# The first loads of a weight gradient: half of slice 1's X goes to a hardware queue, slice 0's narrow G to the software queue

## Chip, core and metric

The kernel runs on one core of one Trainium2 chip. The metric is the device time of one execution in microseconds (us); the time before is the median of four runs.

Engines are named as in the profile: PE multiplies matrices, PEld is its weight load (it overlaps PE), DVE and ACT copy, cast and add, POOL issues the loads of the software queue and SP and ACT those of the hardware queues. DMA engines, 16 of them, move the data of all queues.

## What is computed

```python
batch, m, k, n = 16, 512, 1024, 768
# input: (batch, m, k) float32, grad_output: (batch, m, n) float32
grad_weight = np.einsum('bmk,bmn->kn', input, grad_output)
```

With X as 8192 x 1024 and G as 8192 x 768 this is the product X^T G, 1024 x 768, summed over 8192 rows.

## The kernel before

**Slices.** The 8192 rows are cut into 64 slices (S) of 128 rows. A slice of X is 128 x 1024, a slice of G 128 x 768. Matmuls are in bfloat16 with float32 sums; inputs arrive in float32, so every slice has to be cast.

**Three parts of the output.** The first 512 columns of the output ("wide", columns of G below NA) are made in 8 groups of 128 rows: four groups are part A (they read the first half of X), four are part B (the second half of X). The last 256 columns ("narrow") are made turned over, with narrow G as the weights and X as the moving data, in 4 groups: part N. N's groups take the second half of X first. So a slice costs 4 matmuls in each of A, B and N, each 128 x 128 by 128 x 512, and 12 in all.

**Banks and the order.** There are 8 banks to sum in and 12 groups. The list ORDER (lines 17 to 20) says in which order parts are worked: "A2" brings part A up to slice 2 (slices are counted from 0, so that is slices 0 and 1), and a "!" closes it, that is, its banks are copied (first time, lines 120 to 124, DVE and ACT in turns) or added (later, line 118, DVE) to sums in SBUF and go back to the end of the list of free banks. Before: A1! N1 B2! N2 A2 N3! and so on. The instructions of PE, DVE and ACT run in the order in which they are written (line 67).

**Loads.** Two ways lead in. SP and ACT each own a hardware queue, which copies float32 as it is: slice 0 comes this way (lines 70 to 75), wide G and then narrow G on SP, the two halves of X on ACT, and DVE and ACT cast it (line 106, called from lines 108 to 115). POOL owns the software queue, which casts to bfloat16 on the way: slices 1 to 63 come this way (lines 90 to 97), G before X, and slice 1's X in two halves, the second first. A software load is issued when the one eight places before it has landed; up to eight are under way.

**Before and after.** PE first runs 12 matmuls on constants (line 81) while the first loads are under way. At the end the last 14 slices of A and B are summed group by group (lines 228 to 240), and each group is stored as it is ready.

Of the kernel before, what the change touches and what calls it, by code (L numbers as in the profile page):

```python
# [8 lines left out]
P = 128  # L9
NA = 512  # L10
# [4 lines left out]


ORDER = (
    "A1! N1 B2! N2 A2 N3! A3 B3 A4! B5 N5 B6! N7 A6 N8! A9! B10 N9 B12! N12! A12! "
    "B15 AB17! n17! AB26! n26! AB41! n41! AB47 A50! B50! N64!"
).split()  # L20

# [5 lines left out]
def kernel(  # L27
# [6 lines left out]
    nc = tc.nc  # L34
    bf16 = mybir.dt.bfloat16
    f32 = mybir.dt.float32

    B, M, K = input.shape
    _, _, N = grad_output.shape
    S = B * M // P  # L40
# [5 lines left out]
    X = input.rearrange("b m k -> (b m) k")  # L46
    G = grad_output.rearrange("b m n -> (b m) n")
    OUT = out.rearrange("(ks p) n -> p ks n", p=P)

    head = ctx.enter_context(tc.tile_pool(name="head", bufs=1))  # L50
    xg = ctx.enter_context(tc.tile_pool(name="xg", bufs=XBUFS))
# [10 lines left out]
    xs = [None] * S  # L62
    gwide = [None] * S
    gnarrow = [None] * S
# [2 lines left out]
    ctx.enter_context(tc.manual_schedule(engines={E.PE, E.DVE, E.Activation}))  # L67


    xf = head.tile([P, K], f32, name="xf")  # L70
    gf = head.tile([P, N], f32, name="gf")
    nc.sync.dma_start(out=gf[:, 0:NA], in_=G[0:P, 0:NA])
    nc.scalar.dma_start(out=xf[:, 0:NA], in_=X[0:P, 0:NA])
    nc.sync.dma_start(out=gf[:, NA:N], in_=G[0:P, NA:N])
    nc.scalar.dma_start(out=xf[:, NA:K], in_=X[0:P, NA:K])


    ones = nc.const_aps.tensor(1.0, (P, P), bf16)
# [8 lines left out]
        )  # L87


    for s in range(1, S):  # L90
        gt = xg.tile([P, N], bf16, name="gt")
        nc.gpsimd.dma_start(out=gt, in_=G[s * P : (s + 1) * P, :])  # L92
        xs[s] = xg.tile([P, K], bf16, name="xt")
        for c0, c1 in ((NA, K), (0, NA)) if s == 1 else ((0, K),):
            nc.gpsimd.dma_start(out=xs[s][:, c0:c1], in_=X[s * P : (s + 1) * P, c0:c1])  # L95
        gwide[s] = gt[:, 0:NA]
        gnarrow[s] = gt[:, NA:N]

    xs[0] = head.tile([P, K], bf16, name="x0")
    g0 = head.tile([P, N], bf16, name="g0")  # L100
    gwide[0] = g0[:, 0:NA]
    gnarrow[0] = g0[:, NA:N]

    def round_by(engine, dst, src, c0, c1):
        copy = nc.vector.tensor_copy if engine == "DVE" else nc.scalar.copy
        copy(out=dst[:, c0:c1], in_=src[:, c0:c1])  # L106

    round_by("DVE", g0, gf, 0, 304)
    round_by("ACT", g0, gf, 304, NA)
    for k in range(0, KS // 2, 2):  # L110
        round_by("DVE", xs[0], xf, k * P, (k + 1) * P)
        round_by("ACT", xs[0], xf, (k + 1) * P, (k + 2) * P)
    round_by("DVE", g0, gf, NA, N)
    round_by("DVE", xs[0], xf, NA, 6 * P)
    round_by("ACT", xs[0], xf, 6 * P, K)

    def add_out(dst, src):
        nc.vector.tensor_add(out=dst, in0=src, in1=dst)  # L118
# [68 lines left out]
    def slice_by_slice(names, upto, close):  # L187
        while any(parts[n].done < upto for n in names):
            for n in names:
                part = parts[n]  # L190
                s = part.done
                if s == upto:
                    continue
                part.done += 1
                first = not part.banks
                for i in range(len(part.groups)):
                    if first:
                        open_bank(part, i)
                for i in range(len(part.groups)):
                    add_slice(part, i, s, first, close and s == upto - 1)  # L200

    def bank_by_bank(part, upto):
        first = part.done
        part.done = upto
        for i in range(len(part.groups)):
            open_bank(part, i)
            for s in range(first, upto):
                add_slice(part, i, s, s == first, s == upto - 1)

    for step in ORDER:  # L210
        close = step.endswith("!")
        names = step.rstrip("!").rstrip("0123456789")
        upto = int(step.rstrip("!").lstrip("ABNn"))
        if names.islower():
            bank_by_bank(parts[names.upper()], upto)
        else:
            slice_by_slice(names, upto, close)

    rows_of = out.rearrange("(b r) n -> r b n", r=SQ)
    for a in range(P // SQ):  # L220
        c = NA + a * NT * SQ
        nc.scalar.dma_start(
            out=rows_of[:, :, c : c + NT * SQ],
            in_=turned[a * SQ : (a + 1) * SQ].rearrange("p b r t -> p b (r t)"),
# [3 lines left out]
    for k in range(KS):  # L228
        slices = range(parts["A" if k < KS // 2 else "B"].done, S)
        pieces = [(0, NA)] if k < KS - 1 else [(0, 256), (256, 384), (384, NA)]  # L230
        for c0, c1 in pieces:
            name = free.pop(0)
# [38 lines left out]
```

## Time and profile before

| | us |
|---|---|
| median of 4 runs (176.39 to 176.66) | 176.52 |
| profiled execution, its own time | 176.26 |
| its span (first to last instruction) | 174.5 |
| PE busy | 169.3 |
| first matmul on data (A, slice 0) starts | 4.87 |
| last load of the software queue issued by POOL | 137.0 |
| bytes read from HBM | 58.72 MB |

The span is what the trace covers; the time of the execution has 1.8 us more around it. The granted clock of TensorE is 0.999. Of the DMA engines' time, 90.7% of the span goes to the software queue's packets and 4.4% and 3.9% to the two hardware queues. In rows of the profile, xf and gf are the float32 tiles of slice 0, x and g their bfloat16 copies, and xt and gt the bfloat16 tiles of the software queue.

### The profile page before, as it was taken

What the parts mean: (1) busy time and instruction counts of PE and PEld (TensorE: products, weight loads), DVE (VectorE), ACT (ScalarE), POOL (GpSimd) and SP (SyncE); (2) the same over time, 40 slices, a digit from 0 to 9 for tenths busy, and PEclk for the clock granted to TensorE, in tenths of its full rate; (3) what the DMA queues carried; (4) which work ended last, traced back from release to release, by engine and by line L of the source; (5) the groups of instructions that cost most, each with busy time, mean ns of one, the idle gap of its engine ahead of it and who ended that gap; (6) DMA issues with size and microseconds to landing.
All of it is one profiled execution on the core that took longest, in us unless ns stands there. A gap on an engine that the chain in (4) does not pass through costs nothing.

```text
span 174.5 us, 2012 instructions
## 1 busy us (share of the span) xinstructions
PE 169.3 (97%) x793; PEld 78.0 (45%) x808; DVE 60.9 (35%) x101; ACT 5.6 (3%) x11; POOL 67.4 (39%) x131
## 2 busy tenths in 40 slices
PE   8899999999999999999999999999999999999993
PEld 3344444444444444444444444444444444444463
DVE  0645582882940039300000662200460003932122
ACT  2540000000000000000000000000000000000000
POOL 7544444444445444444444444444264200000000
PEclk9999999999999999999999999999999999999999
DMA  5999999999999999999999999999999991084913
GB/s 159 224 208 209 208 208 208 209 208 208 208 209 209 207 208 209 209 209 208 208 208 209 207 211 207 208 208 208 208 208 209 208 207 22 0 188 130 225 62 120
DMA packets 25336, 33.09 MB, mean 190 GB/s; under 512 B 6512, under 2 KB 16880, under 8 KB 25328
## 3 DMA queue, kind: packets, MB, share of 16 engines
q0 software_dynamic: 18288, 28.91, 90.7%
q1 hardware_dynamic: 2592, 2.49, 4.4%
q10 hardware_dynamic: 4448, 1.57, 3.9%
q8 instruction: 6, 0.10, 0.2%
q14 instruction: 2, 0.02, 0.0%
HBM read 58.72 MB, written 3.15 MB: 355 GB/s over the span
## 4 chain that ended last, share of the span: by engine, by line
PE 80%; DMA 15%; POOL 2%; issue 1%; DVE 0%; POOLq 0%
PE bank L127 53%; PE bank L134 27%; DMA xt<-in_input_dram 15%; POOL gt L92 1%; POOL xt L95 1%; DVE acc L118 0%; POOLq L255 0%
## 5 line engine op out<-in xcount | busy, mean ns | idle before, releaser
L127 PE MATMUL bank<-gt,xt 128*128 128x512 bf16 (+2 forms) x523 | 110.6, 368 | 0.6 <-DMA xt<-in_input_dram 0.2
L127 PEld LDWEIGHTS <-xt 128*128 128x128 bf16 x532 | 50.8, 98 | 58.8 <-DMA xt<-in_input_dram 1.2
L118 DVE TENSOR_TENSOR acc<-bank,acc 128x512 f32<-128x512 f32 (+2 forms) x62 | 37.9, 665 | 73.8 <-PE bank L127 73.4
L134 PE MATMUL bank<-xt,gt 128*128 128x512 bf16 x246 | 55.9, 379 | 0.3
L95 POOL DMA_DIRECT2D xt<-in_input_dram x64 | 33.9, 531 | 37.6 <-DMA xt<-in_input_dram 36.1
L92 POOL DMA_DIRECT2D gt<-in_grad_output_dram x63 | 33.6, 533 | 32.4 <-DMA gt<-in_grad_output_dram 26.0
L134 PEld LDWEIGHTS <-gt 128*128 128x128 bf16 x252 | 24.6, 98 | 29.9 <-issue 0.4
L118 DVE TENSOR_TENSOR acct<-bank,acct 128x512 f32<-128x512 f32 x24 | 15.7, 681 | 30.1 <-PE bank L134 30.0
L81 PE MATMUL bank<-const-bfloat16-1.0 128*128 128x512 bf16 (+1 forms) x12 | 3.6, 468 | 0.8 <-PEq L255 0.8
L122 DVE COPY acc<-bank 128x512 f32<-128x512 f32 x4 | 2.6, 684 | 1.1 <-PE bank L127 1.1
L178 DVE STREAM_TRANSPOSE turned<-acct 128x512 f32<-128x512 f32 x4 | 2.9, 714 | 0.1
L81 PEld LDWEIGHTS <-const-bfloat16-1.0 128*128 128x128 bf16 x12 | 1.4, 124 | 2.8 <-issue 2.4
L127 PE MATMUL bank<-g,x 128*128 128x512 bf16 x8 | 2.1, 380 | 0.5 <-DVE x L106 0.5
L124 ACT COPY acc<-bank 128x512 f32<-128x512 f32 x4 | 2.1, 586 | 1.4 <-PE bank L127 1.4
L106 DVE CAST g<-gf 128x304 bf16<-128x304 f32 (+1 forms) x2 | 0.6, 318 | 4.3 <-DMA gf<-in_grad_output_dram 4.3
L122 DVE COPY acct<-bank 128x512 f32<-128x512 f32 x2 | 1.3, 686 | 1.3 <-PE bank L134 1.3
L127 PEld LDWEIGHTS <-x 128*128 128x128 bf16 x8 | 0.8, 97 | 1.3 <-DVE x L106 0.7
L106 ACT ACT_TABLE_LOAD x1 | 1.3, 1283 | 1.7 <-PEq L255 1.7
L124 ACT COPY acct<-bank 128x512 f32<-128x512 f32 x2 | 1.1, 589 | 1.6 <-PE bank L134 1.6
L134 PE MATMUL bank<-x,g 128*128 128x512 bf16 x4 | 1.0, 377 | 0.1
L106 ACT CAST x<-xf 128x128 bf16<-128x128 f32 (+1 forms) x3 | 0.9, 330 | 0.4 <-DMA xf<-in_input_dram 0.4
L106 DVE CAST x<-xf 128x128 bf16<-128x128 f32 (+1 forms) x3 | 0.8, 295 | 0.2 <-DMA xf<-in_input_dram 0.2
(6 smaller groups left out, 1.2 us busy)
## 6 DMA issues: line engine op xcount, KB each, us to landing
xt<-in_input_dram POOLq DMA_DIRECT2D x62, 256.0 KB, 8.5
gt<-in_grad_output_dram POOLq DMA_DIRECT2D x63, 192.0 KB, 8.5
out_dram<-acc SPq DMA_DIRECT2D x13, 128.0 KB, 3.0
out_dram<-turned ACTq DMA_DIRECT2D x4, 256.0 KB, 3.5
xf<-in_input_dram ACTq DMA_DIRECT2D x2, 256.0 KB, 4.1
gf<-in_grad_output_dram SPq DMA_DIRECT2D x1, 256.0 KB, 3.6
xt<-in_input_dram POOLq DMA_DIRECT2D x2, 128.0 KB, 5.7
out_dram<-acc SPq DMA_DIRECT2D x1, 256.0 KB, 2.0
```

Source lines behind the costliest of these rows:

```text
L81: nc.tensor.matmul(wps[:, 0:cols], ones, nc.const_aps.tensor(1.0, (P, cols), bf16), start=True, stop=True,)
L92: nc.gpsimd.dma_start(out=gt, in_=G[s * P : (s + 1) * P, :])
L95: nc.gpsimd.dma_start(out=xs[s][:, c0:c1], in_=X[s * P : (s + 1) * P, c0:c1])
L106: copy(out=dst[:, c0:c1], in_=src[:, c0:c1])
L118: nc.vector.tensor_add(out=dst, in0=src, in1=dst)
L122: nc.vector.tensor_copy(out=dst, in_=src)
L124: nc.scalar.copy(out=dst, in_=src)
L127: nc.tensor.matmul(bank, xs[s][:, k * P : (k + 1) * P], gwide[s][:, c0:c1], start=start, stop=stop)
L134: nc.tensor.matmul(bank, gnarrow[s].rearrange("p (r t) -> p t r", t=NT)[:, t], xs[s][:, h * NA : (h + 1) * NA], start=start, stop=stop,)
L178: nc.vector.transpose(out=turned[:, h * hb : (h + 1) * hb, :, t], in_=dst.rearrange("p (b r) -> p b r", r=SQ),)
```

## The change

SP's hardware queue still brings slice 0's wide G first; its second load is now the second half of slice 1's X (float32, rows of 2 KB) in place of slice 0's narrow G (rows of 1 KB). ACT's queue is unchanged. The software queue starts with slice 0's narrow G, then slice 1's G and the first half of slice 1's X; from slice 2 on it is as before. Slice 1's second half of X is cast by DVE and ACT, and these casts stand in their order behind the evictions of A1!. Narrow G of slice 0 needs no cast any more. In ORDER a step B1 stands between A1! and N1, so that PE works A, B, N on slice 0 where it was A, N, B; N then sums in the banks that A has left. Slice 1's X no longer uses a buffer of the ring of X tiles.

```diff
 ORDER = (
-    "A1! N1 B2! N2 A2 N3! A3 B3 A4! B5 N5 B6! N7 A6 N8! A9! B10 N9 B12! N12! A12! "
+    "A1! B1 N1 B2! N2 A2 N3! A3 B3 A4! B5 N5 B6! N7 A6 N8! A9! B10 N9 B12! N12! A12! "
...
-    xf = head.tile([P, K], f32, name="xf")
-    gf = head.tile([P, N], f32, name="gf")
-    nc.sync.dma_start(out=gf[:, 0:NA], in_=G[0:P, 0:NA])
-    nc.scalar.dma_start(out=xf[:, 0:NA], in_=X[0:P, 0:NA])
-    nc.sync.dma_start(out=gf[:, NA:N], in_=G[0:P, NA:N])
-    nc.scalar.dma_start(out=xf[:, NA:K], in_=X[0:P, NA:K])
+    xf = [head.tile([P, K], f32, name=f"xf{s}") for s in range(2)]
+    gf = head.tile([P, NA], f32, name="gf")
+    nc.sync.dma_start(out=gf, in_=G[0:P, 0:NA])
+    nc.scalar.dma_start(out=xf[0][:, 0:NA], in_=X[0:P, 0:NA])
+    nc.sync.dma_start(out=xf[1][:, NA:K], in_=X[P : 2 * P, NA:K])
+    nc.scalar.dma_start(out=xf[0][:, NA:K], in_=X[0:P, NA:K])
...
-    for s in range(1, S):
-        gt = xg.tile([P, N], bf16, name="gt")
-        nc.gpsimd.dma_start(out=gt, in_=G[s * P : (s + 1) * P, :])
-        xs[s] = xg.tile([P, K], bf16, name="xt")
-        for c0, c1 in ((NA, K), (0, NA)) if s == 1 else ((0, K),):
-            nc.gpsimd.dma_start(out=xs[s][:, c0:c1], in_=X[s * P : (s + 1) * P, c0:c1])
+    for s in range(S):
+        pool = head if s == 0 else xg
+        gt = pool.tile([P, N], bf16, name="gt")
+        pool = head if s < 2 else xg
+        xs[s] = pool.tile([P, K], bf16, name=f"x{s}" if s < 2 else "xt")
         gwide[s] = gt[:, 0:NA]
         gnarrow[s] = gt[:, NA:N]
...
+        g0 = NA if s == 0 else 0
+        nc.gpsimd.dma_start(out=gt[:, g0:N], in_=G[s * P : (s + 1) * P, g0:N])
+        if s > 0:
+            x1 = NA if s == 1 else K
+            nc.gpsimd.dma_start(out=xs[s][:, 0:x1], in_=X[s * P : (s + 1) * P, 0:x1])
...
-    round_by("DVE", g0, gf, NA, N)
-    round_by("DVE", xs[0], xf, NA, 6 * P)
-    round_by("ACT", xs[0], xf, 6 * P, K)
+    round_by("DVE", xs[0], xf[0], NA, 6 * P)
+    round_by("ACT", xs[0], xf[0], 6 * P, K)
...
-    for step in ORDER:
+    for i, step in enumerate(ORDER):
+        if i == 1:
+            round_by("DVE", xs[1], xf[1], NA, 6 * P)
+            round_by("ACT", xs[1], xf[1], 6 * P, K)
```

More of the change, by code (lines that the diff above doesn't have):

```diff
@@ L87 @@
         )
-    for s in range(1, S):
-        gt = xg.tile([P, N], bf16, name="gt")
-        nc.gpsimd.dma_start(out=gt, in_=G[s * P : (s + 1) * P, :])
-        xs[s] = xg.tile([P, K], bf16, name="xt")
-        for c0, c1 in ((NA, K), (0, NA)) if s == 1 else ((0, K),):
-            nc.gpsimd.dma_start(out=xs[s][:, c0:c1], in_=X[s * P : (s + 1) * P, c0:c1])
+    for s in range(S):
[3 more added lines that the diff above has]
+        xs[s] = pool.tile([P, K], bf16, name=f"x{s}" if s < 2 else "xt")
         gwide[s] = gt[:, 0:NA]
         gnarrow[s] = gt[:, NA:N]
[L99 to L102, printed above, removed]
+        g0 = NA if s == 0 else 0
[3 more added lines that the diff above has]
+            nc.gpsimd.dma_start(out=xs[s][:, 0:x1], in_=X[s * P : (s + 1) * P, 0:x1])
     def round_by(engine, dst, src, c0, c1):
@@ L106, in round_by @@
         copy(out=dst[:, c0:c1], in_=src[:, c0:c1])
-    round_by("DVE", g0, gf, 0, 304)
-    round_by("ACT", g0, gf, 304, NA)
+    round_by("DVE", gwide[0], gf, 0, 304)
+    round_by("ACT", gwide[0], gf, 304, NA)
     for k in range(0, KS // 2, 2):
-        round_by("DVE", xs[0], xf, k * P, (k + 1) * P)
-        round_by("ACT", xs[0], xf, (k + 1) * P, (k + 2) * P)
-    round_by("DVE", g0, gf, NA, N)
-    round_by("DVE", xs[0], xf, NA, 6 * P)
-    round_by("ACT", xs[0], xf, 6 * P, K)
+        round_by("DVE", xs[0], xf[0], k * P, (k + 1) * P)
+        round_by("ACT", xs[0], xf[0], (k + 1) * P, (k + 2) * P)
+    round_by("DVE", xs[0], xf[0], NA, 6 * P)
+    round_by("ACT", xs[0], xf[0], 6 * P, K)
     def add_out(dst, src):
```

## The prediction

> **What bounds the kernel now.** I read the busy shares first, then the chain of waits, then PE's stalls one by one, then the data queues of the first 8 us.
>
> ```profile
> PE 169.3 (97%) x793; PEld 78.0 (45%) x808; DVE 60.9 (35%) x101; ACT 5.6 (3%) x11; POOL 67.4 (39%) x131
> ```
>
> ```profile
> 4.48 8.04 DMA xt<-in_input_dram
> 12.53 0.28 issue
> 12.81 8.55 DMA xt<-in_input_dram
> 21.36 0.28 issue
> 21.64 9.04 DMA xt<-in_input_dram
> 30.68 0.05 issue
> 30.73 1.04 PE bank L127 x4
> ```
>
> PE is busy 97% of the span, and the chain that ended last has two parts. Up to 30.68 us it runs over software-queue loads: an X load lands, the next issue that waited for its semaphore goes out, and that one lands 9 us later. From 30.73 us to the last add at 171.73 us it is PE alone, with no wait. So whatever the change does counts by one thing: when the matmul that now starts at 30.73 us (step B12, slice 11) can start. It starts when slice 11's X has landed (30.68 us). Everything behind it is 141 us of matmuls that the change leaves as they are.
>
> ```profile
> 4.87 1.04 PE L127 MATMUL bank<-g,x 128*128 128x512 bf16 x4 [0.52 <-DVE x L106]
> 6.01 1.02 PE L134 MATMUL bank<-x,g 128*128 128x512 bf16 x4
> 6.87 1.03 PE L127 MATMUL bank<-g,x 128*128 128x512 bf16 x4
> 7.73 1.03 PE L127 MATMUL bank<-gt,xt 128*128 128x512 bf16 x4
> ...
> 30.73 1.04 PE L127 MATMUL bank<-gt,xt 128*128 128x512 bf16 x4 [0.16 <-DMA xt<-in_input_dram]
> ```
>
> (PE's instructions in order of time.) Matmuls start 0.216 us apart, so four take 0.86 us. From the single starts, PE loses between 4.87 and 30.73 us: 0.27 us before N1 (6.01), 0.05 at 10.38, 0.10 at 14.79, 0.07 at 19.18 and 0.32 at 30.73; 0.81 us in all. The last four each begin right behind the landing of X of slice 2 (10.33), 4 (14.74), 6 (19.14) and 11 (30.68). Gaps of 0.43 us at every 50th matmul are missing records, not stalls. That 0.81 us is all that any change in the loads can win once the first matmul has started.
>
> The first stall is this one:
>
> ```profile
> 5.55 0.40 ACT L106 CAST x<-xf 128x256 bf16<-128x256 f32 x1 [0.45 <-DMA xf<-in_input_dram]
> 5.55 0.29 DVE L106 CAST x<-xf 128x256 bf16<-128x256 f32 x1 [0.24 <-DMA xf<-in_input_dram]
> ```
>
> The second half of slice 0's X lands at 5.53 us, the casts end at 5.84 on DVE and 5.95 on ACT, and N1 needs both.
>
> **The data queues.** Busy time by stretch (length, engines, granted clock, DMA share, GB/s):
>
> ```profile
> 3.00:4.00 1.00, 1.00 (x5) 0.36 (x4) 0.00 (x0) 0.00 (x0) 1.00 (x3) 1.00 0.97 328
> 4.00:4.80 0.80, 0.35 (x4) 0.16 (x2) 0.46 (x3) 0.46 (x2) 0.80 (x3) 1.00 1.09 407
> ...
> 6.00:8.00 2.00, 1.99 (x10) 0.92 (x10) 1.04 (x2) 0.93 (x2) 0.77 (x2) 1.00 1.17 190
> ```
>
> GB/s counts bytes written. Up to 4.8 us the hardware queues copy float32, so 407 written is 407 read. Afterwards the software queue writes bfloat16: 190 (208 in the slices of the steady stretch) written is 380 to 416 read. So a byte costs the engines the same on either queue. The packet records say it finer: a 2 KB row is followed by the next on its engine after 80 ns on both kinds of queue, a 1 KB row (narrow G, hardware) after 42 ns, a 3 KB row after 116 ns. They also show the order: an engine does wide G and the first half of X, then the 8 rows of narrow G, then the 8 of the second half of X, and its first software packet (4.82 to 5.16 us, engine by engine) starts some 6 ns after its last hardware packet. The software queue, issued from 1.23 us on, stands behind the hardware queues.
>
> **The change, part by part.** Let d be the shift of the software stream at slice 11's X.
>
> (1) Hardware queues: SP's second load is 256 KB (half of X of slice 1) in place of 128 KB of narrow G. Per engine 8 rows of 80 ns for 8 of 42 ns: +0.30 us; from the stretch at 407 GB/s 131 KB are +0.32 us, at the 328 of 3 to 4 us +0.40. I take +0.32. Two things move with it. The second half of slice 0's X, served behind SP's second load, lands at 5.83 to 5.85 us and not 5.53. And the software queue starts 0.3 us later on each engine.
>
> (2) Software queue: out goes half of X of slice 1 (8 rows of 80 ns an engine, 0.65 us), in comes narrow G of slice 0 (1 KB read, 512 B written). No such row runs in this queue. By bytes read it is like the hardware's narrow row, 42 ns, 0.34 us; from above, a packet that costs what the 1 KB-written one does, 80 ns, 0.64 us. So -0.31 us to 0.00. I take 46 ns: the row that reads the same bytes is the nearest, and software packets of 2, 3 and 4 KB read go at 80, 116 and 156 ns, a line that has almost no fixed part. That is -0.28 us. The number of issues on POOL (each 0.53 us) and the eight loads in flight stay the same, so nothing else in the stream moves.
>
> d = +0.32 - 0.28, about **+0.03 us** (between 0.00 and +0.40 by these ends). In other words: slices 0 to 11 must all have been read before that matmul, the same bytes at the same rate, and only their order among slices 0 and 1 changes.
>
> (3) PE order A1 B1 N1 B2 for A1 N1 B1 B2. B1 needs the late half of X, which N1 needed too. Casts start at 5.85, DVE's ends at 6.14, and with 0.06 us to the weight load (5.84 to 5.90 now) B1 starts at 6.20, where N1 now starts at 6.01; ACT's half (6.25) is wanted at 6.6. So PE is 0.19 us later and not earlier: N1 7.06, B2 7.93, N2 8.79, A2 9.65, N3 10.52. Narrow G lands near 6.2 to 6.4 (first software load now 6.43 us, 0.93 us of packets; later start +0.3, shorter by 0.6), well before 7.06.
>
> (4) Casts removed: DVE's narrow-G cast (0.29 us at 5.01), while DVE then waits for X anyway: nothing. Casts added: slice 1's half, DVE 0.29, ACT 0.40. They stand behind A1's evictions (2 x 0.64 on DVE, 2 x 0.53 on ACT, from 6.06, for DVE starts the next 0.08 us before an end, and from 6.25), so DVE 7.34 to 7.63, ACT 7.31 to 7.71, with their data landed near 5.8. B2 loads weights at 7.72: 0.05 us of wait at most. Behind them stand B2's evictions, wanted from 8.3: free. N1 now takes A1's banks: third bank free at 7.34, wanted at 7.49. This cover is thin; 0.3 us more on the casts would put 0.2 us on N1 or B2.
>
> (5) What becomes of PE's lag: it meets the old stalls. At 10.38 the lag is 0.14, at 14.79 it has eaten the wait of 0.10 and 0.04 is left, at 19.18 nothing. Without any wait for loads PE could be at the B12 matmul at 30.73 - 0.54 + 0.19 = 30.38 us; the load says 30.73 + d. The later one rules, so the lag costs nothing until B1 is another 0.35 us late, and no gain in the stream beyond 0.35 us is usable.
>
> Sum: the profiled execution took 176.26 us (span 174.5); +0.03 makes 176.29. The median of the runs is 176.52, 0.26 above the profiled one, so the forecast is **176.55 us**: no change. A difference below 0.2% (0.35 us) is about what a measurement of this kernel can't tell from none.
>
> **The rivals.** *Small packets hold up the software queue (slower).* Place: narrow G at the head of the queue. For: its X half at the head, the load it replaces, was itself slow to land: the last engine's landing came 1.05 us after wide G's (6.43 to 7.48), the next half's 0.65 later, and single packets there took up to 280 ns for 98. Against: the median engine lost only 0.07. Price: 0.65 to 1.05 us for narrow G where I put 0.37, so d of +0.31 to +0.71; it leaves the 0.2% at about 86 ns a packet. With 0.50 it gives 177.05 us.
>
> *The stream gets ahead (faster).* The same hiccup read the other way: without that half in the software queue up to 0.40 us of it is gone for good. For: two engines carry the delay on to 23.5 us (last landings 0.4 to 0.5 behind the median). Against: slice 11's last landing is another engine's, delayed by a 0.9 us instruction fetch at 23.75 us (its landings trail the others' by 0.5 us from then on). Capped by PE at 0.35, or at 0.40 if the engines happen to serve slice 0's half first, so that B1 isn't late: 176.15 us, at the edge of the 0.2%.
>
> *The queues share (PE becomes the bound).* If software packets mix with the longer hardware queue, the second half of slice 0's X is late by another 8 x 80 ns, B1 starts near 6.84, PE reaches the B12 matmul at 31.02: +0.29 us, 176.8. Against: 16 of 16 engines hand over cleanly now. The Trainium skill ("DMA: Bandwidth & Descriptors", Queues, rings and completion order) says that an engine goes round-robin between the queues that have work, a whole packet of descriptors at a time; by that rule this case is the regular one, and the trace doesn't bear it out for these loads unless the software descriptors were late.
>
> *That it does as its order suggests* (B1 covering N1's wait) needs the late half of X on time; 0.27 us is the most there, and the load of slice 11 takes it back: this is the forecast's own time.
>
> **How the numbers follow.** Forecast 0.52; sharing 0.09, also within 0.2%; small packets 0.22; stream ahead 0.15, of it 0.13 beyond the edge; 0.02 for a bank or cast wait over 0.35 us, on the slow side. So faster 0.13, same 0.63, slower 0.24. The likeliest case's own range is 176.3 to 176.9 (d from -0.2, when the fetch falls on an engine that is further ahead, to +0.4). To leave no more than 2 in 10 out it has to reach the capped gain and most of the small-packet case: 176.1 to 177.1.
>
> **What would show it.** In the changed kernel: second half of slice 0's X cast at about 5.85 (not 5.55); software packets from 5.1 to 5.5; B1 at about 6.2, N1 at about 7.06; X of slice 11 landing at 30.6 to 30.9, PE released by it, and no stall after. It is wrong if slice 11's X lands before 30.4 or after 31.05, if PE waits at B12 for nothing (its own lag ruled), or if software packets start at 4.8 again.

## The result, and the profile after

The changed kernel takes 176.85 us (median of 44 runs, 176.41 to 177.22), the kernel before on the same chips 176.49 us (65 runs, 176.15 to 177.22). The ratio is 1.0018, 95% interval 1.0012 to 1.0023: 0.32 us slower, from 0.21 to 0.41. That is inside the 0.2% within which I called a difference "the same", but with so many runs it can be told from nothing.

The profiled execution of the changed kernel took 176.83 us, its span is 175.1 us (before: 176.26 and 174.5). The shares of the chain that ended last, from the page of the changed kernel:

```profile
PE 94%; DMA 3%; issue 1%; DVE 0%; ACTq 0%
```

Before, 15% of the chain were loads, up to 30.68 us. Now the chain follows PE back to the start. The first part of the chain, in order of time (start, length, what):

```profile
1.19 5.35 DMA xf<-in_input_dram
6.54 0.02 issue
6.56 0.30 DVE x L106
6.87 0.05 issue
6.91 1.04 PE bank L126 x4
7.95 0.86 PE bank L133 x4
```

The load is the late half of slice 0's X on ACT's queue. It lands at 6.54 us, where it landed at 5.53 before; B1, the matmuls of line 126 at 6.91 us, waits for its cast. PE's own instructions:

```profile
4.89 1.16 PE L126 MATMUL bank<-gt,x 128*128 128x512 bf16 x4
6.91 1.04 PE L126 MATMUL bank<-gt,x 128*128 128x512 bf16 x4 [0.86 <-DVE x L106]
7.79 1.03 PE L133 MATMUL bank<-x,gt 128*128 128x512 bf16 x4
```

PE loses 1.03 us ahead of B1. Until 30 us it loses nothing more but 0.05 us, so the old small stalls are eaten. Then slice 11, from the timeline:

```profile
31.30 0.55 PEld L126 LDWEIGHTS <-xt 128*128 128x128 bf16 x4 [0.49 <-DMA xt<-in_input_dram]
```

X of slice 11 lands at 31.26 us (30.68 before) and, by the single starts, B12's matmul starts at 31.31 (30.73 before), after a stall of 0.17 us. From there to the end there is no wait in either kernel: 0.58 us at this matmul is 0.57 us in the times of the two profiled executions. Without that load PE would have been there at 31.14. So two things run late at once, counted from the 30.73 us at which B12 started before: the stream by 0.58 us and PE by 0.41, and PE's lag alone would have made most of the difference of this pair. The profiled execution of before lies near the lower end of its runs, that of the changed kernel at its median, so 0.57 in this pair stands for 0.32.

Why both are late is seen in the stretches of the first 8 us (length, engines, granted clock, DMA share, GB/s written), changed kernel:

```profile
3.00:4.00 1.00, 1.00 (x4) 0.31 (x3) 0.05 (x1) 0.05 (x1) 1.00 (x3) 1.00 1.06 375
4.00:4.80 0.80, 0.80 (x5) 0.37 (x4) 0.66 (x3) 0.71 (x3) 0.80 (x3) 1.00 0.98 271
4.80:5.20 0.40, 0.40 (x4) 0.24 (x3) 0.00 (x0) 0.00 (x0) 0.40 (x2) 1.00 0.81 200
```

From 4 to 4.8 us the hardware queues wrote 407 GB/s before; now they write 271, though the DMA engines are busy all the time (0.98; 1.09 before, where packets overlap): the packets take longer. The packet records say by how much. Read rate in GB/s, in half microseconds from the given start (a software packet counts twice its written bytes):

```
start, us            3.5  4.0  4.5  5.0  5.5  6.0  6.5  7.0
before               381  381  389  418  401  315  369  397
changed              389  307  217  240  233  313  377  414
```

By 6.75 us the kernel before had read 1524 KB and the changed one 1365 KB; 159 KB are 0.39 us at the full rate. Packets of 2 KB on ACT's queue last 84 ns at the median in both kernels, but in the changed kernel from 4.5 to 6 us their mean is 139 to 147 ns and the longest 489; the first three packets of slice 1's G take 236 to 678 ns, 352 in the middle, for 135. From 7 us on both kernels read near the full rate, 416 GB/s, and what was lost by then is carried to slice 11.

### The profile page after: what moved, and what is told of

Its sections match the earlier page's. It is cut to its first block, busy times and chain, and to the rows that moved or that the text cites. A ratio compares the mean times of both kernels' runs of the same rounds, so it can differ in the third digit from the quotient of the medians.

```text
span 175.1 us, 2013 instructions
## 1 busy us (share of the span) xinstructions
PE 169.8 (97%) x793; PEld 78.2 (45%) x808; DVE 60.9 (35%) x101; ACT 5.9 (3%) x12; POOL 67.5 (39%) x131
## 4 chain that ended last, share of the span: by engine, by line
PE 94%; DMA 3%; issue 1%; DVE 0%; ACTq 0%
PE bank L126 63%; PE bank L133 31%; DMA xf<-in_input_dram 3%; ACTq L74 0%; DVE x L106 0%; DVE acc L117 0%
## 5 line engine op out<-in xcount | busy, mean ns | idle before, releaser
L126 PE MATMUL bank<-gt,xt 128*128 128x512 bf16 (+2 forms) x515 | 108.5, 367 | 0.5
L126 PEld LDWEIGHTS <-xt 128*128 128x128 bf16 x524 | 50.0, 98 | 57.6 <-DMA xt<-in_input_dram 0.8
L133 PE MATMUL bank<-xt,gt 128*128 128x512 bf16 x242 | 54.9, 379 | 0.3
L102 POOL DMA_DIRECT2D xt<-in_input_dram x62 | 32.9, 530 | 38.5 <-DMA xt<-in_input_dram 36.2
L99 POOL DMA_DIRECT2D gt<-in_grad_output_dram x64 | 34.2, 534 | 32.4 <-DMA gt<-in_grad_output_dram 26.2
L133 PEld LDWEIGHTS <-gt 128*128 128x128 bf16 x256 | 25.1, 98 | 30.2 <-issue 0.2
L126 PE MATMUL bank<-gt,x 128*128 128x512 bf16 x16 | 4.2, 388 | 0.9 <-DVE x L106 0.9
L82 PE MATMUL bank<-const-bfloat16-1.0 128*128 128x512 bf16 (+1 forms) x12 | 4.3, 547 | 0.8 <-PEq L257 0.8
L126 PEld LDWEIGHTS <-x 128*128 128x128 bf16 x16 | 1.5, 104 | 2.9 <-DVE x L106 1.4
L133 PE MATMUL bank<-x,gt 128*128 128x512 bf16 x8 | 2.1, 379 | 0.0
```

What stands on the lines that cost most here:

```text
L82: nc.tensor.matmul(wps[:, 0:cols], ones, nc.const_aps.tensor(1.0, (P, cols), bf16), start=True, stop=True,)
L99: nc.gpsimd.dma_start(out=gt[:, g0:N], in_=G[s * P : (s + 1) * P, g0:N])
L102: nc.gpsimd.dma_start(out=xs[s][:, 0:x1], in_=X[s * P : (s + 1) * P, 0:x1])
L126: nc.tensor.matmul(bank, xs[s][:, k * P : (k + 1) * P], gwide[s][:, c0:c1], start=start, stop=stop)
L133: nc.tensor.matmul(bank, gnarrow[s].rearrange("p (r t) -> p t r", t=NT)[:, t], xs[s][:, h * NA : (h + 1) * NA], start=start, stop=stop,)
```

## The experiments

All ratios are to the kernel before, timed on the same chip in the same turns. The last columns are from one profiled execution each, in us: when the last engine had landed the late half of slice 0's X, slice 1's G and slice 11's X; and when B12's matmul on slice 11 started (counted back from the last matmul).

| kernel | ratio, interval | late half | G of slice 1 | X of slice 11 | B12 |
|---|---|---|---|---|---|
| before | 1 | 5.53 | 6.43 | 30.68 | 30.73 |
| changed | 1.0018, 1.0012 to 1.0023 | 6.54 | 8.17 | 31.26 | 31.31 |
| order_alone | 0.9996, 0.9987 to 1.0005 | 5.48 | 6.39 | 30.62 | 30.67 |
| loads_alone | 1.0038, 1.0026 to 1.0051 | 6.83 | 8.47 | 31.41 | 31.77 |
| narrow_alone | 1.0048, 1.0035 to 1.0060 | 5.01 | 8.00 | 31.60 | 31.64 |
| half_x_alone | 1.0024, 1.0015 to 1.0033 | 5.75 | 7.02 | 30.79 | 30.84 |
| other_half | 1.0023, 1.0012 to 1.0034 | 6.30 | 7.81 | 30.98 | 31.03 |
| no_narrow | 0.9997, 0.9988 to 1.0007 | 4.89 | 5.99 | 30.64 | 30.69 |
| narrow_second | 1.0008, 0.9996 to 1.0019 | 4.97 | 5.93 | 31.03 | 31.08 |
| late_sw | 1.0025, 1.0012 to 1.0039 | 6.44 | 8.02 | 31.03 | 31.08 |
| g1_leads | 1.0024, 1.0015 to 1.0032 | 6.73 | 7.79 | 30.81 | 31.46 |
| narrow_touch | 1.0046, 1.0031 to 1.0060 | 5.06 | 8.04 | 31.36 | 31.62 |
| half_x_third | 1.0009, 0.9998 to 1.0020 | 5.23 | 7.66 | 30.55 | 30.63 |

The last two columns are the check on the reading of the chain. In eight of the twelve kernels below before's row B12 starts 0.04 to 0.05 us after slice 11's X; in the other four (loads_alone, g1_leads, narrow_touch, half_x_third) PE itself comes later. Behind B12 PE waits for nothing, but for 0.07 and 0.11 us at 42.95 us in narrow_alone and narrow_touch, which are taken off in the last column. A landing in this table is that of one execution: in the profile of relaxed_order (told below), whose loads are those of before, slice 11's X landed at 31.28 us, 0.60 later than in before. So a few tenths of a microsecond in that column can be chance, and it is the ratios that say whether a kernel is slower.

### The order, and the loads, each alone

**order_alone**: before, with the new order.

```diff
-    "A1! N1 B2! N2 A2 N3! ...
+    "A1! B1 N1 B2! N2 A2 N3! ...
```

> The kernel before with the new order A1 B1 N1 B2 and its old loads. Theory L (the loads decide, by when slice 11's X lands): the stream of loads is untouched, so the ratio to before is 1.000 within 0.001; B1 takes N1's place at 6.0 us with the same wait. Rival P (the new order costs PE, by A1's banks and the late half of X): most of the change's 0.32 us is here, ratio about 1.0015 to 1.002.

0.9996 (0.9987 to 1.0005): the order alone costs nothing, as theory L said.

**loads_alone**: the changed kernel with the old order (its casts of slice 1 then stand behind N1).

```diff
-    "A1! B1 N1 B2! N2 A2 N3! ...
+    "A1! N1 B2! N2 A2 N3! ...
```

> The changed kernel's loads and casts with the old order A1 N1 B2. Theory L: slow as the changed kernel, ratio 1.0015 to 1.0025, with slice 11's X landing near 31.0 to 31.3 us (30.68 before). Rival P: back to before, 1.000.

1.0038: slower than the changed kernel, which neither theory said. Its profile tells why, PE's instructions:

```profile
4.65 1.04 PE L126 MATMUL bank<-gt,x 128*128 128x512 bf16 x4
7.60 1.04 PE L133 MATMUL bank<-x,gt 128*128 128x512 bf16 x4 [1.91 <-DMA gt<-in_grad_output_dram]
```

N1, line 133, now stands first and waits for narrow G, which lands at 7.55 us at the end of a slow start of the software queue. PE comes to B12 at 31.77, 0.36 us behind slice 11's X. So the new order is no cost but a cover: with these loads it is worth about 0.35 us (1.0038 less 1.0018).

### The two moves of the loads, each alone

**narrow_alone**: before, with narrow G of slice 0 at the head of the software queue, and nothing in its place on SP's.

```diff
-    nc.sync.dma_start(out=gf[:, NA:N], in_=G[0:P, NA:N])
...
+    nc.gpsimd.dma_start(out=g0[:, NA:N], in_=G[0:P, NA:N])
     for s in range(1, S):
...
-    round_by("DVE", g0, gf, NA, N)
```

> The kernel before, with slice 0's narrow G taken from SP's queue to the head of the software queue, nothing put in its place, old order. If 8 small packets an engine cost what they read (42 to 46 ns each) and the software queue only waits for the hardware queue: second half of X lands near 5.2, software packets from about 4.5, ratio 1.000. Rival S (small packets slow): software stream later by 0.3 to 0.7, ratio 1.002 to 1.004. A third way: the software queue has a start of its own near 4.8 to 5.0 whatever the hardware queues do; then engines stand idle from 4.5 and the stream is late by 0.3 to 0.4, ratio about 1.002.

1.0048, the upper end of rival S and beyond, but not for its reason. The narrow packets take 60 ns (software packets with 1 KB written take 98), and no engine is held by them. It is the load behind them: from 4.5 to 5 us, packets of slice 1's G take 501 ns in the mean and up to 1.9 us, and it lands at 8.00 us, later than in before (6.43) though the software queue began 0.7 us earlier (4.08 for 4.82). The stretches of this kernel:

```profile
4.00:4.80 0.80, 0.80 (x5) 0.38 (x4) 0.60 (x3) 0.70 (x3) 0.80 (x3) 1.00 1.46 213
4.80:5.20 0.40, 0.40 (x4) 0.24 (x3) 0.17 (x1) 0.17 (x1) 0.40 (x2) 1.00 0.98 90
5.20:6.00 0.80, 0.80 (x3) 0.30 (x2) 0.57 (x2) 0.25 (x2) 0.75 (x2) 1.00 0.74 120
```

All that is written here after 4.8 us is bfloat16 of the software queue, whose full rate is 208 GB/s: it writes 90 and 120.

**half_x_alone**: the changed kernel with slice 0's narrow G back on SP's queue, half of slice 1's X behind it, and the old order.

```diff
+    nc.sync.dma_start(out=gf[:, NA:N], in_=G[0:P, NA:N])
     nc.sync.dma_start(out=xf[1][:, NA:K], in_=X[P : 2 * P, NA:K])
...
-        nc.gpsimd.dma_start(out=gt[:, g0:N], in_=G[s * P : (s + 1) * P, g0:N])
         if s > 0:
+            nc.gpsimd.dma_start(out=gt, in_=G[s * P : (s + 1) * P, :])
```

> Slice 1's second half of X on SP's queue behind narrow G, which stays there; the software queue begins with slice 1's G; old order. Theory L in the form that the reads of slice 1's half rows beside slice 0's half rows are slow (180 to 290 GB/s from 4.0 to 6.25 us in the changed kernel, 375 to 430 in the kernel before): the same dip here, slice 11's X late by 0.3 to 0.6, ratio 1.0015 to 1.003. Rival S: no dip, bytes only change queues, ratio 1.000.

1.0024 by the time, but there is no dip: 354 to 453 GB/s read from 4 to 6 us, and slice 11's X is 0.11 us late. Theory L in this form falls. The rest of the loss lies elsewhere. From the last matmul to the end of the span it is 3.44 us, 3.02 in before, and SP's waits name it. Before, then half_x_alone:

```profile
SPq L266 <- DMA out_dram<-acc: 0.7, 1, 0.7
```

```profile
SPq L269 <- DMA out_dram<-acc: 1.1, 1, 1.1
```

SP ends the program by waiting for its stores, and here it does so 0.4 us longer, though the last store lands only 0.12 us later (173.69 us, 173.57 in before). The trace shows why. SP waits for eight completion semaphores one after the other, always in the same order, and each wait takes 0.06 us even when the store has long landed. The last store uses the last of the eight in before; half_x_alone has five hardware loads where before has four, the uses have moved on by one, and the last store uses the first of the eight. So seven more waits, 0.43 us, stand behind its landing. From the last landing to the end it is 1.34 us here, 0.96 to 0.97 in the three kernels with three hardware loads (the last store uses the last semaphore but one), and 0.90 to 0.92 in the ten with four. 0.11 and 0.42 us make 0.53, and the two profiled executions differ by 0.54 (176.80 to 176.26).

### What makes the packets slow

Four kernels ask what brings the dip.

**other_half**: the changed kernel with the first half of slice 1's X on SP's queue and the second in the software queue.

```diff
-    nc.sync.dma_start(out=xf[1][:, NA:K], in_=X[P : 2 * P, NA:K])
+    nc.sync.dma_start(out=xf[1][:, 0:NA], in_=X[P : 2 * P, 0:NA])
...
-            x1 = NA if s == 1 else K
-            nc.gpsimd.dma_start(out=xs[s][:, 0:x1], in_=X[s * P : (s + 1) * P, 0:x1])
+            x0 = NA if s == 1 else 0
+            nc.gpsimd.dma_start(out=xs[s][:, x0:K], in_=X[s * P : (s + 1) * P, x0:K])
...
```

> The changed kernel with the FIRST half of slice 1's X on SP's queue and the second half in the software queue (casts moved with it). Theory C (reading the same half of slices 0 and 1 at once, rows 512 KB apart, is what slows the hardware reads from 3.75 to 5 us): packets of the hardware queues go back to 84 ns between 3.75 and 5 us, rate 375 GB/s or more there. Theory H (the narrow load at the head of the software queue brings the slow reads): the dip of 180 to 300 GB/s between 4 and 6.3 us stays, ratio 1.001 to 1.003.

The packets of slice 1's half on SP's queue still take 126 and 119 ns in the mean from 3.5 to 4.5 us, the read rate is 270 GB/s there, and the first packets of slice 1's G take 208 at the median, up to 558. Ratio 1.0023. Theory C falls: it is not the same half of two slices.

**no_narrow**: before without the load of narrow G.

```diff
-    nc.sync.dma_start(out=gf[:, NA:N], in_=G[0:P, NA:N])
...
-    round_by("DVE", g0, gf, NA, N)
+    nc.vector.memset(g0[:, NA:N], 0.0)
```

> The kernel before without the load of slice 0's narrow G (zeros stand in for it, so that part of the sum is left out); nothing else changes, the software queue begins with slice 1's G. Theory H: no dip; software packets from about 4.4 us, slice 11's X 0.3 us earlier than 30.68, ratio 0.9985 to 0.999 or 1.000 if PE is the bound. Theory E (a software queue that starts earlier than about 4.8 us finds its loads not ready, whatever they are): first packets of slice 1's G up to 1.9 us long as with narrow G alone, no gain, ratio 1.000 to 1.003.

0.9997. Slice 1's G runs at its full rate from 4.21 us and lands at 5.99, 0.44 us earlier than before. But the next load, half of slice 1's X, starts with packets of 188 ns at the median and up to 746 (98 when undisturbed); the read rate falls to 221 GB/s from 5.5 to 6 us, and slice 11's X is only 0.04 us earlier. Theory H's "no dip" is wrong, and so is E's that whatever stands first is slow: the second software load suffers. 128 KB less to load were worth nothing.

**narrow_second**: before with narrow G in the software queue behind slice 1's G; new order.

```diff
-    nc.sync.dma_start(out=gf[:, NA:N], in_=G[0:P, NA:N])
...
         nc.gpsimd.dma_start(out=gt, in_=G[s * P : (s + 1) * P, :])
+        if s == 1:
+            nc.gpsimd.dma_start(out=g0[:, NA:N], in_=G[0:P, NA:N])
...
```

> Narrow G of slice 0 in the software queue as in the run with narrow G alone, but second, behind slice 1's G; new order, since narrow G comes later. Theory H in the form that only the head of the queue matters: no dip, slice 11's X within 0.2 us of 30.68, ratio 1.000 to 1.001. If small packets are slow wherever they stand, or the early start is what counts (E): as with narrow G alone, slice 11's X at 31.3 or later, ratio 1.003 to 1.005.

1.0008 (0.9996 to 1.0019): not to be told from before, where narrow G at the head gave 1.0048. Slice 1's G and the narrow rows run undisturbed (135 and 60 ns), and the dip moves on to the half of X behind them (151 ns in the mean from 5.5 to 6 us). Slice 11's X at 31.03 is 0.35 us late in this profile, more than the first theory gave and less than the second. The place at the head matters; in this one profile something else seems to count too.

**late_sw**: the changed kernel, POOL filling a scratch tile for 0.95 us first, which puts its first load 0.39 us later.

```diff
+    idle = head.tile([P, 1024], f32, name="idle")
+    nc.gpsimd.memset(idle, 0.0)
     for s in range(S):
```

> The changed kernel with POOL filling a scratch tile before its first load, so that the software queue begins later. Theory C: the dip between 3.75 and 5 us stays, as it lies on the hardware queues. Theory H or E: with the software loads later the hardware reads run at 375 GB/s or more up to their end near 5.4 us, the late half of slice 0's X lands near 5.85 (6.54 in the changed kernel). The time: no better than the changed kernel if the stream starts after 5.4 us.

Mixed. The hardware packets are at 84 to 90 ns until 4.5 us, where the changed kernel has 102 to 114 in the mean from 4.0; but the late half still lands at 6.44, the first packets of slice 1's G take 328 ns in the mean, and the time is 1.0025. So the start of the software queue is not the whole cause of the dip.

**narrow_touch**: narrow_alone, with a small load that reads from each row of slice 1's G before.

```diff
+    touched = head.tile([P, 8], f32, name="touched")
+    nc.sync.dma_start(out=touched, in_=G[P : 2 * P, 0:8])
```

> The run with narrow G alone at the head of the software queue, with one small load added: SP reads the first 8 numbers of each row of slice 1's G into a scratch tile right behind wide G. Theory F (the first read of a slice's rows is slow, and hidden only for a load that has stood in the queue for long): with the rows touched before, slice 1's G starts at 135 ns a packet, lands near 6.5 us (8.00 without), ratio 1.001 or less in place of 1.0048. If it isn't the first touch but the load's place behind a short one: landing after 7.3, ratio 1.003 or more.

1.0046 and 8.04 us: nothing changed (1.0048 and 8.00). Packets of slice 1's G still take 485 ns in the mean from 4.5 to 5 us. It is not the first touch of those rows.

### Which of the two lags rules

**g1_leads**: the changed kernel with slice 1's G first in the software queue and narrow G second.

```diff
+        if s > 0:
+            nc.gpsimd.dma_start(out=gt, in_=G[s * P : (s + 1) * P, :])
+        if s == 1:
+            nc.gpsimd.dma_start(out=gnarrow[0], in_=G[0:P, NA:N])
-        nc.gpsimd.dma_start(out=gt[:, g0:N], in_=G[s * P : (s + 1) * P, g0:N])
```

> The changed kernel with one thing turned round: slice 1's G leads the software queue and slice 0's narrow G comes second. Theory H (a short load at the head makes the load behind it start slowly): first packets of slice 1's G back at 135 ns, slice 11's X at 30.7 to 30.9 us (31.26 in the changed kernel), ratio to before 1.000 to 1.001. If the place in the queue doesn't matter and the changed kernel's loss is in the hardware queues' half of X: ratio 1.0015 to 1.0025.

Each theory has half of it, the first the landing and the second the time: the first packets of slice 1's G are back at 135 ns (median), slice 11's X lands at 30.81, and the ratio is 1.0024. Its chain:

```profile
1.18 5.55 DMA xf<-in_input_dram
6.73 0.02 issue
6.76 0.31 DVE x L108
7.06 0.05 issue
7.11 1.04 PE bank L128 x4
```

There is no wait at B12 any more. PE lost 1.59 us ahead of B1, because the late half of slice 0's X lands at 6.73, and comes to B12 at 31.46, 0.65 us behind the load. With the stream mended, PE is the bound.

**half_x_third**: the changed kernel with half of slice 1's X on ACT's queue, third, so that slice 0's late half doesn't stand behind it.

```diff
-    nc.sync.dma_start(out=xf[1][:, NA:K], in_=X[P : 2 * P, NA:K])
     nc.scalar.dma_start(out=xf[0][:, NA:K], in_=X[0:P, NA:K])
+    nc.scalar.dma_start(out=xf[1][:, NA:K], in_=X[P : 2 * P, NA:K])
```

> The changed kernel with slice 1's second half of X issued on ACT's queue, third, behind the late half of slice 0's X; SP carries wide G alone. By the bytes nothing moves in the software stream; slice 0's late half no longer stands behind 256 KB and should land near 5.2 to 5.4 us (6.54 in the changed kernel), so PE's own path to the B12 matmul is 30.1 to 30.4 us and cannot rule. If what costs is the stream alone (slow packets of slice 1's half and of the load behind the short one, wherever they are issued): slice 11's X at 31.0 to 31.3, ratio 1.001 to 1.002. If the slow packets come from the two halves of X being read at once on two queues: no dip, slice 11's X at 30.6 to 30.8, ratio 0.9995 to 1.0005.

1.0009 (0.9998 to 1.0020): about half of the changed kernel's loss by the medians, but the interval tells it neither from before nor from the changed kernel. Its first matmuls:

```profile
4.95 1.90 PE L126 MATMUL bank<-gt,x 128*128 128x512 bf16 x8
6.69 1.03 PE L133 MATMUL bank<-x,gt 128*128 128x512 bf16 x4
7.70 1.02 PE L126 MATMUL bank<-gt,x 128*128 128x512 bf16 x4
```

A1 and B1 run without a gap, eight matmuls from 4.95 us, for the late half is there at 5.23. The slow packets remain (slice 1's G starts with 316 ns in the mean, 229 GB/s read from 5.5 to 6 us), though slice 11's X lands at 30.55. The profiled execution (176.16) is the fastest of this kernel's runs (median 176.63), so 30.55 is not its usual landing.

### An order that wants slice 11 later

**relaxed_order**: before, with slices 4, 6 and 11 wanted later.

```diff
-    "A1! N1 B2! N2 A2 N3! A3 B3 A4! B5 N5 B6! N7 A6 N8! A9! B10 N9 B12! N12! A12! "
+    "A1! N1 B2! N2 A2 N3! A3 B3 A4! B4 N4 B5 N5 B6! N6 A6 N8! A9! B10 N9 B11 N11 B12! N12! A12! "
```

> The kernel before, loads untouched, with an order that wants slices 4, 6 and 11 later: A4! B4 N4 B5 N5 B6! N6 A6 N8! A9! B10 N9 B11 N11 B12! in place of A4! B5 N5 B6! N7 A6 N8! A9! B10 N9 B12!. If the wait for slice 11 alone sets the time, as the reading of the chain says, the stalls at 14.79, 19.18 and 30.73 us (0.49 us) go and the ratio is 0.9972 to 0.998. If later waits for slices or banks take their place: 0.999 to 1.000.

1.0071: 177.80 us to 176.46, far slower. In its profile PE never waits for a load behind N1; it waits for banks instead. From the list of PE's waits (waited for: total, times, longest):

```profile
PE bank L127 <- DVE acc L118: 0.4, 2, 0.2
PE bank L134 <- DVE acc L118: 0.2, 1, 0.2
```

The list shows only the idle part. The matmuls around the first of these waits:

```profile
15.32 1.01 PE L134 MATMUL bank<-xt,gt 128*128 128x512 bf16 x3
16.54 0.38 PE L134 MATMUL bank<-xt,gt 128*128 128x512 bf16 x1 [0.22 <-DVE acc L118]
```

From the starts, PE loses 0.58 us at each of three places (15.95 to 16.54, 20.84 to 21.44, 36.09 to 36.69), 1.74 in all: the steps put in between a close and the next opening had been the time in which DVE added up the banks. 1.74 less the 0.49 of load waits that it was to remove is 1.25, and the ratio gives 1.25 us (0.0071 of 176.46; 1.01 to 1.50 by its interval). That fits load waits worth what the prediction said and a cover that cost more; it doesn't measure the load waits by themselves. (In the profiled execution itself the first matmuls ran at half pace, told at the end, which also hides load waits; the sum of the medians is the better evidence.)

## Why the prediction was right, and where it wasn't

The forecast, 176.55 us and no change, is 0.30 us under the measured median, and that lies inside the range and, by the point estimate, inside the 0.2%. What held is the frame: what the change does counts only by when B12 can start, and that is the later of two arrivals. That the number came so near is luck in part. By one of the prediction's own signs its account was wrong: slice 11's X landed at 31.26 us, past the 31.05 that it named. Both arrivals were late, and the time stayed in the range because the two lags run side by side up to B12 and don't add. (The terms +0.32 and -0.28 also make +0.04, not the +0.03 of the sum.)

**Step (1), the hardware queues, failed for PE's arrival.** It priced 131 KB more at 407 GB/s, so that slice 0's late half lands at 5.83 to 5.85 us. It landed at 6.54: 1.01 us later than before in place of 0.30. The rate was not to be had: 217 to 307 GB/s read from 4 to 6 us in place of 381 to 418. "The same bytes at the same rate" was true of the steady stretch and not of the one in which the change acts.

**Step (2), the small packets, failed for the stream.** It was right about the narrow rows: they take 60 ns at the median, where a software row of twice the size takes 98. What it left out is that the load behind them starts slowly; narrow_alone puts 0.91 us of delay at B12 on that in its profile (31.64 to 30.73) and 1.0048 in its time, where the prices of the steps give +0.03 us (0.37 in, 0.34 out). With slice 1's G at the head instead and step (1)'s loads as they are (g1_leads), slice 11's X is 0.13 us late. So, by these profiles, most of the stream's lag (d of +0.58 in place of +0.03) came in with this step.

**Step (3)** had the mechanism and the wrong size with step (1): B1 at 6.20, N1 at 7.06; measured 6.91 and 7.79. Narrow G was given 6.2 to 6.4 and landed at 7.27, and still ahead of N1.

**Step (4)** held. Slice 1's casts, from 7.83 on ACT and 7.97 on DVE, end ahead of B2, which follows N1 without a gap at 8.65, and no bank is waited for.

**Step (5)** held in form. It gave PE 0.35 us of room before its lag costs; B1 came 0.71 us later than planned, so the room was used up, and PE and the stream were 0.17 us apart at B12. g1_leads shows what that means: mending the stream alone gains nothing.

**The rivals.** None came true as told. The one in which small packets hold up the software queue had the place and the size: narrow G at the head, d of +0.31 to +0.71 (+0.58 in the profile) and 177.05 us (176.85), for a chance of 0.22. But it is the load behind the narrow rows that is slow, and not the rows.

The one in which the queues share, with PE as the bound, put B1 at 6.84 (6.91) and the time at 176.8 (176.85), for a chance of 0.09; that is a coincidence. Software packets run from 5.02 us and the last hardware packet starts at 6.10, but, as far as the records tell, on different DMA engines. They name no engine, but a load's end on each of them shows as a packet of 4 bytes. No software packet starts before the first of the 16 ends of ACT's second load (5.02 us; the last is at 6.19), and 4 to 8 ns after 13 of the 16 one does; it is 16 of 16 in before and in g1_leads. So the late half was held up by slow packets of the hardware queues, its own and those of SP's load ahead of it, and not by software packets in between. The rule that it was weighed against, in the Trainium skill ("DMA: Bandwidth & Descriptors", Queues, rings and completion order), that an engine goes round-robin between queues with work, agrees with the two kernels that have a third load on one hardware queue, half_x_third and half_x_alone: a software packet starts 4 to 8 ns after all 16 ends of ACT's second load, ahead of most of that third load, whose packets run to 6.27 and 7.37 us. Serving the loads in the order of their arrival would look the same.

That the stream gets ahead isn't seen.

**What stays open** is why packets take up to 15 times their time between 4 and 6.5 us. It isn't the same half of two slices (other_half), nor the first touch of the rows (narrow_touch), nor only the moment at which the software queue starts (late_sw, no_narrow), nor software packets in between those of the hardware queues, and narrow rows at the head make it worse (narrow_alone against narrow_second). Each profile is one execution. The Trainium skill ("DMA: Bandwidth & Descriptors", Latency and other measured facts) gives accesses of HBM 0.2 us on average and 2 us at high load; packets of 1.9 and 2.0 us (narrow_alone, narrow_touch) are of that size, but no run shows that it is memory they waited for.

## What to carry to other kernels

Don't price a load of the first microseconds at the steady rate: here the read rate from 4 to 6 us fell from 381 to 418 GB/s to 217 to 307 with the change, and each way of moving loads in that stretch cost something or gave nothing that could be told from none, 0.9997 to 1.0048. When two arrivals meet at one instruction, find both before mending either, and put a load that a wait hangs on ahead of one that nobody needs yet, as half_x_third does (late half at 5.23 us in place of 6.54). An order that removes a wait for data may have been the cover of a wait for banks: count the time from each close to the next use of that bank before steps are put in between.

## What the hardware showed that I had not expected

The software load behind the narrow rows starts slowly when these stand at the head. Slice 1's G then landed at 7.66 to 8.47 us in all seven kernels of that kind, whether 24 or 32 hardware rows of 2 KB an engine went ahead. With slice 1's G itself at the head it landed at 5.93 to 7.02 us, and at 7.79 only in g1_leads, which has half of X on SP's queue besides. Slow packets aren't only found there: in no_narrow, with no narrow rows at all, the second software load began with packets of up to 746 ns.

The start of the full pace varies between executions of much the same beginning. The matmuls on constants start at 0.78 us in every profile, 0.43 us apart; the step to 0.216 us came between 3.3 us (before) and 6.6 us (relaxed_order), and in narrow_alone and order_alone the four matmuls of A1 ran at the slow pace, until 6.2 us or later. The granted clock reads 1.00 in these stretches too, so that column doesn't show the step. So the twelve matmuls ahead of the data don't always outlast the slow pace; A1 at half pace is 0.86 us longer, of which B1's or N1's wait for its load hides a part.
